# A hybrid LRU/GLA layer on one core: the kernel's scheduler takes a longer figure for split-precision matmuls

## The chip, the cores and the metric

One core of a Trainium2 chip runs the whole program in one launch. The metric is the device time in microseconds; the median of three runs is given. The engines are TensorE (PE in the profile, its weight loads PEld), VectorE (DVE), ScalarE (ACT), GpSimd (POOL) and SyncE (SP), which issues most DMAs.

## The reference, cut to what matters

One layer is applied to two token groups (128 prompt tokens and 512 latent tokens, 640 in all, width 1024), with shared weights:

```python
h = rmsnorm(x, ng[0]) * (1.0 + sc1) + sh1          # sc, sh, g: from silu(c) @ w_mod
z = h @ w_in                                        # 1024 x 7200
zx, zg, q, k, v, g, lr, ga, gb = split(z)
xc = conv4(zx); hf, hb = rg_lru_scan(xc) in both directions   # block-diagonal gates, sigmoid, exp, sqrt, scan
y_a = ((hf + hb) * gelu(zg)) @ lru_up
o = gla_chunked(q, k, v, decay from lr) in both directions, 4 heads
y_b = (rmsnorm(o) * silu(g)) @ gla_up
m = (sigmoid(ga) * y_a + sigmoid(gb) * y_b) @ w_out
x = x + g1 * rmsnorm(m, ng[1])
h = rmsnorm(x, ng[2]) * (1.0 + sc2) + sh2
x = x + g2 * rmsnorm(square(relu(h @ mlp_w1)) @ mlp_w2, ng[3])
```

Besides the tokens, the final LRU and GLA states of the prompt are returned. Everything is float32.

## The kernel before

All large matrix products are done in split precision: a float32 operand is cast to the type fp32r (its high half: `whi`, `HH`, `ah`) by ScalarE, VectorE subtracts that from the original (its low half: `wlo`, `HL`, `al`), and three matmuls on fp32r operands (high x high, high x low, low x high) are summed in PSUM. The 640 tokens are the columns of most matmuls, as two halves of 320; the v projection has 256 columns, the output projection and the second MLP product 512. Weights come as 1 MB loads into two `raw` tiles and are split into four `whi`/`wlo` buffers.

The program is first recorded and only then issued. The function `tile_hybrid_layer` calls engine operations through `Port` objects; each call becomes an `Op` in the `Recorder`. The recorded order is a list of units, one for each weight piece: first the startup (modulation, norms, transposes), then the input projection with its zx, q, k, v, g, zg pieces, the gates and up-projections, the output projection (`out_pass`), and the MLP (`w1_units`, `w2_units`). Between the units' halves the planner `slot` puts stages of side chains: `lru_chain` (operand split `xs`, gate matmuls into `aux` PSUM tiles, sigmoid reads `r`, exchange by DMA, tanh, exp, sqrt, scans), `gla_chain` (heads, in nine stages), the modulation chains, and the splits of the results. `dense` and `aux` are two PSUM pools of two tiles each: unit results and side-chain results. The planner's budgets are constants (`us=0.01 * (c1 - c0)`, `FILL`) and don't use the lengths that this change touches.

Then `Recorder.order` (L222) makes the order in which every engine gets its instructions. It is a list scheduler: it simulates the five engines in time, with a length for each instruction from `Recorder.cost` (L133), a lag between engines, tile buffers that come free, table switches of ScalarE (`SWITCH_US`, 1.28 us) and a slower TensorE where it has been idle. At each step the engine that can start first takes, of its instructions that are ready, the one of lowest rank (its place in the recorded order; weight splits get a lead of `SPLIT_AHEAD` places; ScalarE prefers instructions that need no table switch). `issue` (L331) then issues all instructions in the order of these simulated times, and on the chip each engine runs its queue in that order, waiting for semaphores where its data isn't there yet. All instructions are recorded as being of line L340, so the profile is read by tile names.

Of the kernel before, what the change touches and what calls it, by code (L numbers as in the profile page):

```python
# [56 lines left out]
def _dims(ap):  # L57
    n = 1
    for _, k in ap.ap[1:]:
        n *= k  # L60
    return n
# [48 lines left out]
class Recorder:  # L110
# [21 lines left out]
    @staticmethod  # L132
    def cost(eng, name, args, kw, out):  # L133
        n = _dims(out)
        if eng == "PE":
            if name == "transpose":
                return max(0.05, n * 2 / 2400)
            if args[1].dtype == F32R:
                return max(n / 2400 + 0.0025, 0.106)
            if out.ap[0][1] <= 32 and n >= 128:  # L140
                return n / 2400 + 0.0025
            return max(0.213, n * 4 / 2400)
        aps = [a for a in list(args[1:]) + list(kw.values()) if hasattr(a, "ap")]
        scalars = sum(_dims(a) == 1 for a in aps) if n > 1 else 0
        sbuf = all(a.space == bass.MemoryType.SB for a in aps)
        if eng == "ACT":
            if name == "dma_start":
                return 0.1
            return (0.093 if sbuf else 0.051) + n / 1200 + 0.094 * scalars
        if eng == "DVE":  # L150
            if name == "reciprocal":
                return 6.25e-3 * n
            fast = name in ("tensor_copy", "tensor_scalar", "memset") and sbuf and out.space == bass.MemoryType.SB
            return 0.068 + n / (1920 if fast else 960) + 0.061 * scalars
        if eng == "POOL":
            if name == "dma_start":
                return 1.0
            if name in ("memset", "affine_select"):
                return 0.03 + n * 0.0009
            if name == "tensor_copy":  # L160
                return 0.1 + n * 0.0034
            return 0.1 + n * (0.008 if name == "tensor_scalar" and n < 64 else 0.0022) + (0.35 if kw.get("op") == OP.pow else 0.06)
        return 0.63 if kw["in_"].space == bass.MemoryType.SB else 0.5
# [1517 lines left out]
```

## Time and profile before

| | us |
|---|---|
| median of 3 runs | 1164.29 (1162.61 to 1165.95) |
| the profiled execution: its time | 1160.65 |
| the profiled execution: its span, first to last instruction | 1158.9 |
| TensorE busy in the span | 1131.3 |
| VectorE, ScalarE, GpSimd busy | 755.6, 557.8, 80.1 |

The span is shorter than the execution's own time by 1.75 us, which lies around the first and last instruction. A matmul's shown length is longer than the distance to the next one, because matmuls overlap; the distance is read from a run of many. "Idle before" is the time in which an engine had nothing running, and behind the arrow stands what ended it.

### The profile page before, as it was taken

To read this page: it belongs to the slowest core of one execution; us is meant where nothing else is said; L and a number is where in the kernel's file an instruction comes from. 1 tells how busy PE (TensorE), PEld (TensorE's weight loads), DVE (VectorE), ACT (ScalarE), POOL (GpSimd) and SP (SyncE) were. 2 spreads that over 40 slices of the span, in tenths; PEclk is the share of its full clock that TensorE was granted. 3 is DMA by queue.
4 is the path that set the end of the run, shared out by engine and by line. 5 is a ranking of instruction groups with operands and counts; after the bars stand their busy time and mean duration, and the time that the engine had idled before them with its cause. 6 is when DMAs were issued, how large, how long until landed. Compare 5 with 4: busy or idle time off the path is not lost.

```text
span 1158.9 us, 17719 instructions
## 1 busy us (share of the span) xinstructions
PE 1131.3 (98%) x7188; PEld 1064.3 (92%) x7188; DVE 755.6 (65%) x1147; ACT 557.8 (48%) x882; POOL 80.1 (7%) x152
## 2 busy tenths in 40 slices
PE   6999999999999999999999999999999999999996
PEld 5899899999999999999999879999999989999995
DVE  4687885966557557549968389885444555555546
ACT  6387989994657668213432388422222222222222
POOL 3135112000000000000000021000000000000001
PEclk9999999999999999999999999999999999999999
DMA  9835445332121312245535356532222222222202
GB/s 296 253 78 142 132 110 132 93 104 77 52 92 40 102 60 83 64 158 207 191 128 182 112 179 199 192 118 74 73 73 74 73 73 73 78 81 86 85 1 90
DMA packets 101009, 130.63 MB, mean 113 GB/s; under 512 B 7790, under 2 KB 77632, under 8 KB 100928
## 3 DMA queue, kind: packets, MB, share of 16 engines
q1 hardware_dynamic: 98880, 127.61, 35.6%
q0 software_dynamic: 2048, 1.90, 0.7%
q8 instruction: 56, 0.92, 0.3%
q14 instruction: 25, 0.20, 0.1%
HBM read 117.94 MB, written 3.68 MB: 105 GB/s over the span
## 4 chain that ended last, share of the span: by engine, by line
PE 78%; DVE 8%; ACT 5%; DMA 5%; issue 2%; POOL 1%; SPq 0%; DVEq 0%; POOLq 0%; ACTq 0%
PE dense L340 62%; PE aux L340 16%; DVE i L340 2%; DVE th L340 2%; DMA i<-r 1%; DVE wlo L340 1%; DMA modw<-in_w_mod_dram 1%; ACT L340 1%; ACT r L340 1%; ACT th L340 1%; DMA raw<-in_w_in_dram 1%; DMA w2raw<-in_gla_w_dram 1%; DMA r<-r 1%; ACT whi L340 1%; ACT L339 0%
## 5 line engine op out<-in xcount | busy, mean ns | idle before, releaser
L340 ACT CAST whi<-raw 128x1024 fp32r<-128x1024 f32 (+1 forms) x159 | 164.5, 1038 | 394.2 <-PE dense L340 363.6
L340 DVE TENSOR_TENSOR wlo<-raw,whi 128x1024 fp32r<-128x1024 f32 x154 | 188.1, 1223 | 173.5 <-ACT whi L340 173.1
L340 PE MATMUL dense<-HH,whi 128*128 128x320 f32 x768 | 178.1, 312 | 0.2 <-ACT vc L340 0.2
L340 PE MATMUL dense<-HL,whi 128*128 128x320 f32 x768 | 176.1, 310 | 0.0
L340 PE MATMUL dense<-HH,wlo 128*128 128x320 f32 x752 | 172.4, 309 | 0.0
L340 PEld LDWEIGHTS dense<-HH,whi 128*128 128x128 f32 x768 | 128.4, 188 | 2.1 <-issue 0.8
L340 PEld LDWEIGHTS dense<-HL,whi 128*128 128x128 f32 x768 | 128.9, 188 | 0.0
L340 PEld LDWEIGHTS dense<-HH,wlo 128*128 128x128 f32 x752 | 125.9, 188 | 0.0
L340 PE MATMUL dense<-H2H,whi 128*128 128x320 f32 (+2 forms) x496 | 116.8, 309 | 0.0
L340 PE MATMUL dense<-H2H,wlo 128*128 128x320 f32 (+2 forms) x496 | 116.4, 308 | 0.0
L340 PE MATMUL dense<-H2L,whi 128*128 128x320 f32 (+2 forms) x496 | 116.4, 308 | 0.0
L340 PEld LDWEIGHTS dense<-H2H,whi 128*128 128x128 f32 x496 | 84.5, 188 | 1.3
L340 PEld LDWEIGHTS dense<-H2L,whi 128*128 128x128 f32 x496 | 84.0, 188 | 0.0
L340 PEld LDWEIGHTS dense<-H2H,wlo 128*128 128x128 f32 x496 | 84.0, 188 | 0.0
L340 DVE SCALAR_TENSOR_TENSOR mac<-mw,cst,mac 128x512 f32<-128x512 f32 x112 | 77.9, 747 | 2.9 <-DMA mw<-in_w_mod_dram 2.7
L340 PE MATMUL dense<-wlo,ah 128*128 128x512 f32 (+1 forms) x192 | 75.3, 392 | 0.0
L340 PE MATMUL dense<-whi,ah 128*128 128x512 f32 (+1 forms) x192 | 75.3, 392 | 0.0
L340 PE MATMUL dense<-whi,al 128*128 128x512 f32 (+1 forms) x192 | 75.3, 392 | 0.0
L340 PE MATMUL aux<-wlo,ah 128*128 128x512 f32 (+1 forms) x132 | 51.7, 392 | 0.0
L340 PE MATMUL aux<-whi,ah 128*128 128x512 f32 (+1 forms) x132 | 51.7, 391 | 0.0
L340 PE MATMUL aux<-whi,al 128*128 128x512 f32 (+1 forms) x132 | 51.6, 391 | 0.0
L340 PE MATMUL dense<-whi,HH 128*128 128x256 f32 x160 | 45.0, 281 | 0.0
(311 smaller groups left out, 2172.6 us busy)
## 6 DMA issues: line engine op xcount, KB each, us to landing
raw<-in_mlp_w_dram SPq DMA_DIRECT2D x34, 1024.0 KB, 5.7
raw<-in_w_in_dram SPq DMA_DIRECT2D x24, 1024.0 KB, 5.5
mw<-in_w_mod_dram SPq DMA_DIRECT2D x64, 256.0 KB, 5.6
modw<-in_w_mod_dram SPq DMA_DIRECT2D x32, 256.0 KB, 6.1
raw<-in_w_out_dram SPq DMA_DIRECT2D x8, 1024.0 KB, 4.9
i<-r SPq DMA_DIRECT2D x32, 160.0 KB, 2.6
raw<-in_w_in_dram SPq DMA_DIRECT2D x8, 512.0 KB, 4.0
raw<-in_lru_up_dram SPq DMA_DIRECT2D x4, 1024.0 KB, 5.1
```

Source lines behind the costliest of these rows:

```text
L340: getattr(eng[o.eng], o.name)(*o.args, **o.kw)
```

## The change

`Recorder.cost` returns the planned length in microseconds of one instruction; `n` is the number of columns. For a matmul on fp32r operands it returns another figure:

```diff
             if name == "transpose":
                 return max(0.05, n * 2 / 2400)
             if args[1].dtype == F32R:
-                return max(n / 2400 + 0.0025, 0.106)
+                return max(n / 2200, 0.106)
             if out.ap[0][1] <= 32 and n >= 128:
                 return n / 2400 + 0.0025
             return max(0.213, n * 4 / 2400)
```

Nothing else differs: the same operations are recorded, in the same recorded order, on the same engines and tiles. What can differ is the order in which `order` lets each engine run them, the DMA issues of SyncE and GpSimd among them.

## Rows read from the trace of the kernel before

**Rows 1.** The page's first part: busy time, share of the span, instructions.
```profile
PE 1131.3 (98%) x7188; PEld 1064.3 (92%) x7188; DVE 755.6 (65%) x1147; ACT 557.8 (48%) x882; POOL 80.1 (7%) x152
```
**Rows 2.** Busy time by stretches: PE, PEld, DVE, ACT, POOL, clock, DMA.
```profile
0.00:50.00 50.00, 38.99 (x311) 31.62 (x312) 28.14 (x81) 25.28 (x62) 11.21 (x40) 0.90 0.94 291
...
100.00:265.00 165.00, 160.19 (x1148) 158.41 (x1146) 126.53 (x181) 149.64 (x182) 18.69 (x32) 1.00 0.41 112
265.00:675.00 410.00, 408.91 (x2759) 398.64 (x2758) 268.24 (x405) 198.02 (x359) 11.28 (x9) 1.00 0.35 113
675.00:700.00 25.00, 23.24 (x115) 18.66 (x114) 22.36 (x41) 21.01 (x40) 5.79 (x5) 1.00 0.51 152
700.00:1150.00 450.00, 449.98 (x2521) 407.00 (x2519) 267.71 (x374) 130.16 (x187) 4.90 (x7) 1.00 0.28 89
1150.00:1158.90 8.90, 0.00 (x0) 0.00 (x0) 3.59 (x8) 1.00 (x4) 1.44 (x2) 0.71 0.39 118
```
**Rows 3.** TensorE's waits, whole run: total us, times, longest.
```profile
PE aux L340 <- ACT r L340: 2.9, 3, 1.7
...
PE aux L340 <- DVE xs L340: 1.7, 1, 1.7
...
PE dense L340 <- DVE wlo L340: 0.8, 1, 0.8
PE aux L340 <- DVE nst L340: 0.7, 1, 0.7
PE aux L340 <- DVE nrm L340: 0.6, 1, 0.6
...
PE aux L340 <- DVE ab L340: 0.4, 1, 0.4
PE aux L340 <- ACT nrm L340: 0.4, 1, 0.4
```
**Rows 4.** Chain pieces (320, then 512 columns); then TensorE's groups, 100 to 265 us.
```profile
473.31 63.46 PE dense L340 x432
...
642.75 2.80 PE aux L340 x12
...
L340 PE MATMUL dense<-HL,whi 128*128 128x320 f32 x246 | 56.2, 309 | 0.0
...
L340 PE MATMUL dense<-whi,HH 128*128 128x256 f32 x110 | 30.7, 279 | 0.0
L340 PE MATMUL dense<-wlo,HH 128*128 128x256 f32 x109 | 30.4, 279 | 0.0
...
L340 PE MATMUL aux<-xs,bh 128*128 128x320 f32 x48 | 11.6, 323 | 4.6 <-ACT r L340 2.9 <-DVE xs L340 1.7
```
**Rows 5.** ScalarE's groups from 100 to 265 us: busy us, mean ns, idle.
```profile
L340 ACT ACT_TABLE_LOAD x22 | 28.2, 1283 | 0.4
L340 ACT CAST whi<-raw 128x1024 fp32r<-128x1024 f32 x20 | 20.9, 1048 | 3.5 <-PE dense L340 2.7 <-DMA raw<-in_w_in_dram 0.8
L340 ACT ACTIVATE r<-aux,C 128x640 f32<-128x640 f32 x24 | 18.2, 791 | 0.4 <-PE aux L340 0.3
L339 ACT ACT_TABLE_LOAD x12 | 15.4, 1283 | 0.2
```
**Rows 6.** VectorE's groups from 100 to 265 us.
```profile
L340 DVE TENSOR_TENSOR wlo<-raw,whi 128x1024 fp32r<-128x1024 f32 x20 | 24.4, 1220 | 12.3 <-ACT whi L340 12.3
L340 DVE TENSOR_TENSOR_SCAN i<-r,C,th 128x512 f32<-128x512 f32 x16 | 20.3, 1269 | 0.0
```
**Rows 7.** The chain of waits by line: 100 to 265 us, then 265 to 460.
```profile
by line: DVE i L340 16.7%; DVE th L340 11.4%; issue 9.5%; PE dense L340 8.2%; DMA i<-r 8.0%; ACT L340 6.2%; ACT r L340 5.6%; DVE wlo L340 4.9%; ACT th L340 4.8%; DMA r<-r 4.5%; ACT whi L340 2.3%; DVE xs L340 2.0%; DVE ab L340 1.7%; ACT L339
...
by line: PE dense L340 66.2%; PE aux L340 25.1%; ACT ab L340 1.8%; issue 1.4%; DVE wlo L340 1.2%; DVE ab L340 1.1%; DVE la L340 0.8%; ACT L339 0.7%; DVE zg L340 0.6%; DVE i L340 0.6%; DVE ep L340 0.4%; DVE ex L340 0.2%; DVE bm L340 0.1%; DV
```
**Rows 8.** ScalarE's waits from 100 to 265 us.
```profile
ACT whi L340 <- PE dense L340: 2.7, 5, 0.8
ACT zg L340 <- PE dense L340: 2.6, 1, 2.6
```

## The prediction

> **What bounds the kernel now.** I read the page's first part, then the table by stretches, then TensorE's waits, then what is behind them. The first part says that TensorE is busy 98% of the span [rows 1]; VectorE and ScalarE are far below. So the time is the length of TensorE's work and its idle time, and an order of work can only touch the second. The stretches say where it is [rows 2]: 50.00 - 38.99 = 11.0 us in the first 50 us, 165.00 - 160.19 = 4.8 us from 100 to 265 us, 1.1 us from 265 to 675, 1.8 us from 675 to 700, nothing (0.02 us) from 700 to 1150, and the 8.9 us tail after the last matmul.
>
> The stretch from 100 to 265 us is the one to look at. It holds the LRU chains: ScalarE is busy 149.64 of 165 us there, 91% [rows 2]. TensorE's waits in it are four: three times on ScalarE's reads of the gates' PSUM tiles (r), 2.9 us in all, and once on VectorE's operand split (xs), 1.7 us [rows 3]. The chain of waits through this stretch is VectorE, ScalarE and DMA; dense matmuls are 8.2% of it [rows 7]. From 265 to 460 us, where the GLA chains run, it is the reverse: dense and aux matmuls are 66.2% and 25.1% [rows 7], and the only TensorE waits are two short ones (nst 0.7 us, ab 0.4 us) [rows 3]. From 675 to 700 us, between the output projection and the MLP, TensorE waits for the normalised tiles (nrm) and once for a low half of a weight (wlo) [rows 3].
>
> **The change part by part.** No instruction is added or removed. A matmul on split-precision operands of 320 columns was planned at 320/2400 + 0.0025 = 0.1358 us and is now planned at 320/2200 = 0.1455 us; of 256 columns 0.1092 and 0.1164; of 512 columns 0.2158 and 0.2327. Of 128 columns it stays at the floor of 0.106. The trace's lengths: 63.46 us for 432 matmuls of 320 columns is 146.9 ns each, 2.80 us for 12 of 512 columns is 233 ns [rows 4]. So the new figures are right to 1%, and the old ones were 7 to 8% short.
>
> The Trainium skill speaks against this: "TensorE: Matmul & The Clock Gate", section on the back-to-back issue gap, gives N/2.4 + 2.5 ns for a warm array, which is the old formula to the digit. By it the LRU stretch's matmuls would be 147 us long, TensorE's idle time there would be 18 us and not 4.8, the helpers alone would set the pace, and the whole 10.25 us worked out below would be lost (1175). The trace does not agree: 146.9 ns, and 160.19 us of work.
>
> What the plan does with the number: it walks all engines in simulated time, and each engine takes the first instruction in program order that is ready at that moment. An aux matmul whose operands or PSUM tile are not ready is passed by dense matmuls. With matmuls planned longer, fewer dense ones fit while a helper works, so aux matmuls move forward in TensorE's queue, which on the chip is then followed as it stands. Whether that is good hangs on how true the helpers' planned lengths are, and the trace shows that they are short too. ScalarE: a weight cast is planned at 0.093 + 1024/1200 = 0.946 us and takes 1.048; a gate sigmoid is planned at 0.051 + 640/1200 + 0.094 = 0.678 and takes 0.791; table loads are planned right (1.28) [rows 5]. VectorE: the low half of a weight is planned at 0.068 + 1024/960 = 1.135 and takes 1.220; a scan of 512 is planned at 0.662 and takes 1.269 [rows 6]. So before, everything was planned about 8 to 15% short, TensorE like the rest; the relative error on ScalarE was small. With 34 loads of 1.283 us right and the other 106 us some 13% short (between the cast's 11% and the sigmoid's 17%), ScalarE's 149.6 us were planned as 137.4, 9% short, against 160.19 / 147.2 = 9% for TensorE. Afterwards TensorE is planned right, and the helpers alone are planned short. The plan then expects them earlier, measured in matmuls, than they come.
>
> Term 1, the LRU stretch. It has 1148 matmuls, all split-precision [rows 2]: 110 + 109 + 109 = 328 of 256 columns (two groups of 109, one shown) and 820 of 320 columns [rows 4]. Old plan 820 x 0.1358 + 328 x 0.1092 = 147.2 us, new plan 820 x 0.1455 + 328 x 0.1164 = 157.4 us: 10.25 us more by the unrounded formulas. If the helpers set every position of an aux matmul, they come due 10.25 us of matmuls earlier by the end of the stretch, and TensorE idles 10.25 us more: the upper bound. If they come in program order, ready in time, nothing moves: 0. The 48 gate matmuls of one kind make 24 PSUM tiles [rows 4], and TensorE waited at 4 of them [rows 3]; 4/24 of 10.25 is 1.7 us, and 92% (the chain without dense matmuls [rows 7]) is 9.4 us. I take 3 us, nearer to the first, because at 20 of 24 tiles TensorE found its data ready; some of these have less slack than the shift and will join the four. Queued behind a waiting aux matmul are all dense matmuls, and with them the evacuations and weight casts, so the loss is not made up later: behind 700 us TensorE has no idle time to give back.
>
> Term 2, 675 to 700 us. 115 matmuls [rows 2], 16.9 ns more for one of 512 columns: 1.9 us at most. Two groups of transposes (nrm) waited, 0.6 and 0.4 us [rows 3]; I take half of that, 0.5 us. Term 3, the GLA stretch: helpers hold 100 - 66.2 - 25.1 = 8.7% of the chain, 17 us of 195; 6.6% of that is 1.1 us at most, and I take 0.2.
>
> Costed at nothing: the start, where TensorE works on float32 transposes and modulation sums and on the DMAs behind them, whose planned lengths stay, with the first split-precision matmuls put between (I allow 1 us either way); the MLP, where TensorE never waits and VectorE is busy 268 of 450 us [rows 2], so a split that comes a few us later is still in time; without that cover each late low half would cost about the 0.8 us of the one wait seen [rows 3]. The tail hangs on the last units alone.
>
> Sum: 3.0 + 0.5 + 0.2 = +3.7 us on the profiled execution's 1160.65, 1164.35; the median of the runs shown is 3.64 us above that execution, so 1168.0 in its terms.
>
> **The rivals.** (a) Nothing that can be measured. The order shifts, but slack takes it up: 20 of 24 gate tiles were not waited for, and the chain is TensorE itself outside the LRU stretch. Terms of 0 to 1.5 us: about 1165. Against it: a list order is never moved by exactly nothing, and ScalarE at 91% has little slack. That the order comes out the same on every engine, so that the change does nothing, belongs here too; since every matmul's planned end moves, I hold it for unlikely.
>
> (b) Faster. ScalarE's queue is in order too: in the LRU stretch it stood idle 2.7 us before weight casts and 2.6 us before a zg copy, waiting for dense matmuls that the old plan thought done [rows 8]. With true matmul lengths these go later in ScalarE's queue, and gate reads that stood behind them go earlier. If ScalarE gets those 5.3 us back and the LRU chains end that much sooner, TensorE's 4.8 us of waits there go, and perhaps 1 us at 675: 1164.3 - 5.8, about 1158.5. It decides where the gate reads come more than 1 us earlier, since the mean wait is 4.6/4. Against it: VectorE's scans, planned at half their length, are just as late as before, and one of the four waits is VectorE's.
>
> (c) Slower by more: table switching. 34 table loads take 43.6 us of the stretch [rows 5]. A plan that thinks ScalarE less loaded finds fewer instructions waiting at once and switches more often. Five loads more are 6.4 us on an engine with 15 us to spare. With term 1 that gives 1171 to 1175. It is the upper half of the slower case.
>
> **How the numbers follow.** About 0.3%, 3.5 us, is what a measurement of this kernel can tell from no change. Slower by more, by terms 1 to 3 with or without (c): 0.45, and the likeliest time is 1168. Within it, (a): 0.35. Faster, (b): 0.20. My terms' upper bounds, 10.25 + 1.9 + 1.1 = 13.3 us, give 1177.6; all waits behind 50 us gone, 4.8 + 1.1 + 1.8 = 7.7 us, gives 1156.6. The range of 1158 to 1175 leaves out the outer edges of both. The slower case by itself is 1167 to 1176.
>
> **What would show it.** TensorE's busy time should stay at 1131 us and its matmul count at 7188. Right would be: idle time from 100 to 265 us of 7 to 9 us where it was 4.8, behind gate matmuls that wait for r or xs, and the last LRU step (nst) with fewer dense matmuls ahead of it. The stretch from 700 to 1150 us should be unchanged. Wrong would be fewer than 4.8 us there with ScalarE's waits for dense matmuls gone (b), the same waits at other places (a), or new waits in the MLP for wlo, which I count at nothing. A count of table loads far from 53 would speak for or against (c).

## The result and the profile after

The median went from 1163.51 us (1162.61 to 1165.95, 4 runs, one more than in the table above) to 1184.72 us (1182.5 to 1185.5, 4 runs): a ratio of 1.0176, with a 95% interval of 1.0154 to 1.0197. The change is slower, by 21 us. The forecast was slower by 3.7 us and the range ended at 1175, so the sign came out and the size did not. The profiled execution took 1184.93 us with a span of 1183.2, that is 24.3 us more than the span of before.

The page's first part of the changed kernel, to be held against [rows 1], and its line of ScalarE's table loads at one of the two places that issue them:

```profile
PE 1137.8 (96%) x7188; PEld 1067.9 (90%) x7188; DVE 755.7 (64%) x1147; ACT 569.5 (48%) x891; POOL 80.7 (7%) x152
...
L340 ACT ACT_TABLE_LOAD x43 | 55.2, 1283 | 1.5 <-PEq L1668 0.8
```

TensorE ran the same 7188 matmuls and was busy 6.5 us longer; the other 17.8 us are idle time. ScalarE has 9 instructions more (891 against 882). These are table loads: the page shows 43 here where that of before has 34, and 19 at the other place (L339) in both. VectorE and GpSimd did the same work.

The stretches of the changed kernel, cut so that they hold about the work of [rows 2] (the columns are the same):

```profile
0.00:50.00 50.00, 37.35 (x302) 30.03 (x303) 27.62 (x80) 25.43 (x62) 10.20 (x38) 0.90 0.94 282
50.00:100.00 50.00, 48.65 (x329) 47.74 (x328) 33.09 (x55) 32.58 (x51) 30.53 (x61) 1.00 0.38 101
100.00:284.00 184.00, 165.91 (x1145) 163.01 (x1143) 135.43 (x191) 162.03 (x195) 18.62 (x32) 0.97 0.41 110
284.00:696.00 412.00, 409.59 (x2772) 399.52 (x2773) 263.90 (x399) 194.90 (x353) 8.90 (x7) 1.00 0.35 112
696.00:722.00 26.00, 24.19 (x117) 19.15 (x116) 23.83 (x43) 20.85 (x41) 6.57 (x6) 1.00 0.47 138
722.00:1173.00 451.00, 450.79 (x2521) 407.36 (x2520) 267.50 (x375) 132.48 (x188) 4.66 (x7) 1.00 0.28 90
1173.00:1183.20 10.20, 1.35 (x12) 1.15 (x10) 4.33 (x11) 1.29 (x6) 1.22 (x2) 0.69 0.34 103
```

Some 1145 matmuls of the LRU stretch now take 184 us, where 1148 took 165. TensorE's idle time by stretch, against [rows 2]: 12.7 us at the start (11.0), 1.4 from 50 to 100 us (the stretch that [rows 2] leave out had none), 18.1 in the LRU stretch (4.8), 2.4 in the GLA stretch (1.1), 1.8 in the transition (1.8), 0.2 in the MLP (0.02), and a tail of the same length. So 13.3 of the 17.8 us lie in the LRU stretch. The granted clock has fallen to a mean of 0.97 there; it was 1.00.

TensorE's waits over the whole run of the changed kernel, against [rows 3]:

```profile
PE aux L340 <- ACT r L340: 10.1, 6, 3.2
PE dense L340 <- ACT zp L340: 5.1, 3, 2.9
...
PE aux L340 <- DVE nst L340: 1.8, 1, 1.8
PE aux L340 <- DVE ab L340: 1.7, 2, 1.0
PE dense L340 <- ACT vc L340: 1.4, 1, 1.4
PE aux L340 <- DVE nrm L340: 1.4, 1, 1.4
```

Gate matmuls wait for ScalarE's reads (r) 10.1 us in place of 2.9. New is that dense matmuls wait 5.1 us for ScalarE's evacuation of a dense tile (zp), which [rows 3] don't have at all. Both point at ScalarE, so its waits come next. From 75 us to the last LRU step (nst, at 284 us) they are in the changed kernel:

```profile
ACT th L340 <- POOL p4sp L340: 6.4, 1, 6.4
ACT th L340 <- DMA r<-r: 5.6, 1, 5.6
ACT va L340 <- PE dense L340: 4.2, 1, 4.2
ACT whi L340 <- PE dense L340: 3.5, 5, 0.8
```

and in the kernel before, over the same work (75 to 266 us, which begins 25 us ahead of [rows 8]):

```profile
ACT whi L340 <- PE dense L340: 7.3, 7, 4.4
ACT zg L340 <- PE dense L340: 2.6, 1, 2.6
...
ACT th L340 <- DMA r<-r: 0.9, 2, 0.4
```

Waits for dense matmuls are not what grew: they are 7.7 us in all, and were 10.3 (with 0.4 for va). What is new stands elsewhere. Twice a tanh (th) stands at the head of ScalarE's queue before its data is there, once for a constant that GpSimd makes (p4sp) and once for the exchange by DMA (r). These two are 12.0 us, where the kernel before has 0.9. The timeline of ScalarE in the changed kernel shows the first of them, and what follows (start, us, engine, line, operation, and in brackets the idle time ahead of it):

```profile
86.38 0.73 ACT L340 CAST xs<-xc 64x640 fp32r<-64x640 f32 x1
93.48 1.55 ACT L340 ACTIVATE th<-r,p4sp 128x640 f32<-128x640 f32 x2 [6.38 <-POOL p4sp L340]
95.05 1.28 ACT L339 ACT_TABLE_LOAD   x1
96.34 1.55 ACT L340 ACTIVATE r<-r,n8sp 128x640 f32<-128x640 f32 x2
97.79 0.63 ACT L340 COPY zp<-dense 128x192 f32<-128x192 f32 x2
...
100.22 1.28 ACT L340 ACT_TABLE_LOAD   x1
101.51 0.83 ACT L340 ACTIVATE th<-r,p4sp 128x640 f32<-128x640 f32 x1
102.36 1.28 ACT L340 ACT_TABLE_LOAD   x1
```

In the kernel before the four tanhs stand together, later in the queue and with no wait ahead of them:

```profile
101.38 2.99 ACT L340 ACTIVATE th<-r,p4sp 128x640 f32<-128x640 f32 x4
```

Two tanhs were placed earlier, and a third alone behind them. ScalarE stands still for 6.4 us, then switches tables for one or two instructions at a time, and the copies and casts behind them are late.

### The profile page after: what moved, and what is told of

Read it like the earlier page. It is cut to its first block, busy times and chain, and to the rows that moved or that the text cites. A ratio compares the mean times of both kernels' runs of the same rounds, so it can differ in the third digit from the quotient of the medians.

```text
span 1183.2 us, 17745 instructions
## 1 busy us (share of the span) xinstructions
PE 1137.8 (96%) x7188; PEld 1067.9 (90%) x7188; DVE 755.7 (64%) x1147; ACT 569.5 (48%) x891; POOL 80.7 (7%) x152
## 4 chain that ended last, share of the span: by engine, by line
PE 72%; ACT 12%; DVE 5%; DMA 4%; issue 4%; POOL 2%; SPq 0%; ACTq 0%; DVEq 0%; POOLq 0%
PE dense L340 58%; PE aux L340 14%; ACT L340 3%; DMA modw<-in_w_mod_dram 2%; ACT r L340 2%; ACT th L340 1%; ACT whi L340 1%; ACT L339 1%; POOL spp L340 1%; DMA i<-r 1%; ACT ab L340 1%; DVE i L340 1%; DMA raw<-in_w_in_dram 1%; DVE wlo L340 1%; ACT zg L340 1%
## 5 line engine op out<-in xcount | busy, mean ns | idle before, releaser
L340 PEld LDWEIGHTS dense<-HH,whi 128*128 128x128 f32 x768 | 129.5, 190 | 10.1 <-ACT zp L340 5.9
```

What stands on the lines that cost most here:

```text
L340: getattr(eng[o.eng], o.name)(*o.args, **o.kw)
```

## Did the gate matmuls move in TensorE's queue?

The prediction said that aux matmuls come forward past dense ones. Whether they did can be read from counts: the matmuls that were run from the start to a given gate tile. In the kernel before, gate tiles begin at 204.41, 225.74 and 232.28 us; up to just before these:

```profile
0.00:204.40 204.40, 190.50 (x1387) 182.25 (x1388) 143.84 (x247) 154.47 (x231) 56.66 (x130) 0.97 0.57 162
0.00:225.73 225.73, 211.60 (x1527) 202.80 (x1528) 165.07 (x278) 173.94 (x255) 56.66 (x130) 0.98 0.55 153
0.00:232.27 232.27, 216.46 (x1559) 207.40 (x1559) 171.61 (x291) 180.43 (x263) 56.66 (x130) 0.98 0.55 155
```

In the changed kernel gate tiles begin at 221.04, 243.05 and 251.12 us:

```profile
0.00:221.03 221.03, 194.94 (x1387) 184.63 (x1388) 148.56 (x254) 166.06 (x241) 59.35 (x130) 0.96 0.53 150
0.00:243.04 243.04, 215.72 (x1527) 205.16 (x1528) 167.29 (x285) 186.68 (x267) 59.35 (x130) 0.96 0.51 144
0.00:251.11 251.11, 220.58 (x1559) 209.75 (x1559) 175.11 (x295) 194.65 (x276) 59.35 (x130) 0.97 0.52 146
```

1387, 1527 and 1559 matmuls stand ahead in both kernels. These three gate tiles didn't move in TensorE's queue; they are reached 16.6, 17.3 and 18.8 us later. Of the 18.8, 14.7 are idle time (30.53 - 15.81) and 4.1 longer busy time for the same 1559 matmuls. On ScalarE 276 instructions were run by then and not 263, in 14.2 us more of busy time.

Not all gate tiles stayed. There are 32 of them, of four matmuls each; counted in the same way and taken in order, 20 have as many matmuls ahead as before, 11 have fewer (by 2 to 120) and one has more (by 12). The furthest move is that of two tiles side by side, of which the first began at 160.41 us and begins at 153.40 now; the last LRU step (nst) moved too. Up to just before the tile and before nst, in the kernel before:

```profile
0.00:160.40 160.40, 146.71 (x1067) 138.91 (x1068) 113.51 (x208) 116.54 (x186) 47.34 (x114) 0.97 0.58 166
0.00:265.84 265.84, 249.38 (x1799) 240.03 (x1799) 194.55 (x324) 207.66 (x296) 56.66 (x130) 0.98 0.53 148
```

and in the changed one:

```profile
0.00:153.39 153.39, 131.94 (x947) 122.48 (x948) 100.27 (x189) 104.50 (x171) 47.35 (x110) 0.96 0.59 168
0.00:284.21 284.21, 251.91 (x1772) 240.78 (x1772) 196.35 (x325) 220.04 (x307) 59.35 (x130) 0.96 0.49 138
```

So aux matmuls did come forward, as the prediction said: 120 matmuls for these two tiles, 27 for nst. But most of the wait isn't there. TensorE's timeline has the gate tiles' waits for r, in the last brackets; three of the six are:

```profile
129.65 0.56 PE L340 MATMUL aux<-xs,bh 128*128 128x320 f32 x2 [1.31 <-ACT r L340]
...
193.21 0.56 PE L340 MATMUL aux<-xs,bh 128*128 128x320 f32 x2 [2.71 <-ACT r L340]
...
251.12 0.56 PE L340 MATMUL aux<-xs,bh 128*128 128x320 f32 x2 [3.21 <-ACT r L340]
```

The first is a tile that came forward (by 10 matmuls), the other two stayed. Of the 10.1 us, 3.7 are at three tiles that came forward (1.3 at 129.65, 1.8 at 142.90 and 0.5 at 144.30 us), where the kernel before waited 2.7 us (1.0 for r, 1.7 for xs); 6.4 are at three that stayed (2.7, 0.5 and 3.2). The two tiles that moved by 120 aren't waited for at all. The rest of the 18.1 us in the LRU stretch is 6.4 us before dense matmuls and 1.6 before nst.

## The experiments

Four theories were set against each other. **R** (proportion): what counts is whether the planned lengths of the engines stand in proportion; a true matmul among helpers that are planned short puts the in-order queues out of step with one another. **Q** (ScalarE's queue): the loss is in that queue alone, in its waits at the head and its table loads. **D** (the prediction): positions of aux matmuls in TensorE's queue. **L** (luck): any other order of instructions would have cost as much, the one of before was a lucky one. Ratios are against the kernel before, run on the same chip.

**One engine's queue kept.** Two plans are made; one engine's order is taken from the first and forced on the second:

```diff
+        kept = {e: [o.idx for o in self.plan(first, {}) if o.eng == e] for e in ('ACT',)}
+        return self.plan(second, kept)
```

Run 1 has ScalarE's order as before and plans the rest with the new figure:

> New matmul figure, but ScalarE's queue is kept in the order that the old plan gave it (53 table loads); all other queues are planned around it with the new figure. Theory Q (the loss sits in ScalarE's queue: nine more table loads, 9 x 1.283 = 11.5 us, and two waits at the head of its queue, 6.4 and 5.6 us): within 5 us of the kernel before, 1160 to 1168. Theory D (my prediction's term 1: TensorE's own queue has aux matmuls too early, because the helpers alone are planned short): TensorE's queue is still of the new figure, so 1178 to 1186 stays.

Run 2 has the old figure, and ScalarE's order as in the changed kernel:

> Old matmul figure, but ScalarE's queue is kept in the order that the new plan gave it (62 table loads); all other queues are planned around it with the old figure. Theory Q: the loss comes without the change, 1178 to 1188. Theory D: TensorE's queue is planned with the old figure, so 1163 to 1168.

Run 3 has TensorE's order as before, and the rest with the new figure:

> New matmul figure, but TensorE's queue is kept in the order that the old plan gave it; the others are planned around it with the new figure, which gives ScalarE 57 table loads. Theory D: the loss goes, 1162 to 1167. Theory Q: ScalarE's order is still a new one, four table loads more than before (5.1 us) and whatever head waits it has, so 1169 to 1183.

| run | median us | ratio, interval | table loads |
|---|---|---|---|
| 1 ScalarE as before | 1172.21 | 1.0075 (1.0053 to 1.0096) | 53 |
| 2 ScalarE as after | 1179.57 | 1.0136 (1.0119 to 1.0152) | 62 |
| 3 TensorE as before | 1176.99 | 1.0114 (1.0095 to 1.0134) | 57 |

ScalarE's order carries most of the loss and not all: with the order of before 43% of the loss is left (0.75 of 1.76), and the order of after brings 77% of it to queues that are otherwise planned with the old figure. (The other queues are planned anew around the one that is kept, so neither run has them as they were.) What is left in run 1 is seen at the gate matmuls, which wait 6.7 us for r though ScalarE's order is the old one:

```profile
PE aux L364 <- ACT r L364: 6.7, 4, 3.3
```

ScalarE itself waits 19.6 us for dense matmuls there, from 75 to 285 us:

```profile
ACT va L364 <- PE dense L364: 10.0, 2, 8.4
ACT whi L364 <- PE dense L364: 9.6, 9, 3.9
```

That is more than in the kernel before (10.3), but run 9 below has nearly as much of it, 17.8 us, and no loss, so it doesn't explain what is left:

```profile
ACT whi L344 <- PE dense L344: 12.5, 10, 3.1
ACT va L344 <- PE dense L344: 5.3, 3, 4.3
```

TensorE's order of before leaves 65% of the loss. In run 3 its gate matmuls wait as they do in the changed kernel, 9.4 us:

```profile
PE aux L364 <- ACT r L364: 9.4, 5, 3.9
```

So theory D doesn't hold for most of it: with its own old order TensorE waits all the same, because what it waits for is late. And Q alone doesn't hold either: the order of before, beside a plan with the new figure, still loses 0.75%. Run 1 lies between the ranges that were set for Q and D; runs 2 and 3 lie in Q's.

**Other lengths brought to the true ones too.** Run 4 keeps the new matmul figure and gives GpSimd's smallest operations, with which it makes the constant p4sp, 0.5 us; run 5 makes all the helpers 7% longer, in step with the matmul:

```diff
             # run 4, GpSimd
+            if n <= 16:
+                return 0.5
...
         # run 5, behind o.us = self.cost(...)
+        if eng in ("ACT", "DVE", "POOL") and name != "dma_start":
+            o.us *= 1.07
```

> New matmul figure, and GpSimd's instructions on 16 columns and fewer (the softplus chain behind the tanh's scale p4sp) planned at 0.5 us, about what the trace shows, where they were planned at 0.2 to 0.3. Nothing else. Theory Q, with its start at the tanh that ScalarE's queue has too early: the plan then puts the tanhs later, the 6.4 us wait goes, ScalarE has 54 table loads and not 62, and the time is 1162 to 1170. Theory D: GpSimd's lengths have no part in it, 1180 to 1186.

> New matmul figure, and ScalarE's, VectorE's and GpSimd's planned lengths times 1.07, so that they stand to TensorE's as in the kernel before. Theory R (what counts is that all engines are planned equally short; the matmul alone made true sets the in-order queues against each other): most of the loss goes, 1160 to 1168, with 48 table loads. Theory L (the old plan's order was a lucky one among many; any other order costs 5 to 20 us): 1170 to 1182.

Run 4: 1175.96 us, ratio 1.0106 (1.0088 to 1.0124). The wait for p4sp is gone and 54 table loads are left of 62, yet 60% of the loss stays: less than D's range has and more than Q's. Run 5: 1165.48 us, 1.0021 (1.0007 to 1.0035), 48 loads: 88% of the loss is taken back, with the new matmul figure in place. This lies in R's range.

**Size of the step, and luck.** Run 6 takes `n / 2300`, halfway in the divisor: a matmul of 320 columns is planned 3.3 ns longer than before, where the change adds 9.6. Run 7 takes `n / 2050`, which adds 20.3 ns. Run 8 keeps the old figure and gives each helper instruction a fixed pseudo-random error of up to 3% either way:

```diff
+        o.us *= 1 + 0.03 * (((o.idx * 2654435761 + 1 * 40503) >> 7) % 1024 / 511.5 - 1)
```

> The matmul planned at n / 2300, about half of the change's step (0.139 us for 320 columns, between 0.136 and 0.1455); 53 table loads in the plan. Theory R: about half of the loss, 1170 to 1176. Theory L: no relation to the step's size, anywhere from 1163 to 1185.

> The matmul planned at n / 2050, longer than it is (0.156 us for 320 columns), twice the change's step; 59 table loads in the plan. Theory R: the helpers stand still shorter against TensorE, more is lost than by the change, 1186 to 1200. Theory L: no relation, 1165 to 1185.

> Old matmul figure; each length of ScalarE, VectorE and GpSimd is off by a fixed pseudo-random share between -3% and +3%, with no bias. 58 table loads in the plan, 5 more than before. Theory R: no bias, so little is lost beyond the table loads, 1162 to 1170. Theory L: another order, another 5 to 20 us, 1169 to 1184.

| run | median us | ratio, interval | table loads |
|---|---|---|---|
| 6 3.3 ns added | 1164.71 | 1.0016 (1.0003 to 1.0028) | 53 |
| 7 20.3 ns added | 1199.9 | 1.0315 (1.0293 to 1.0338) | 59 |
| 8 random errors, old figure | 1163.14 | 1.0004 (0.9994 to 1.0014) | 58 |

For 3.3, 9.6 and 20.3 ns the loss is about 2, 21 and 37 us: it grows with the step, and the first third of the step costs less than its share (7 us). Run 6 is a miss for R, which was set to lose 1170 to 1176 there. The order of run 8 is another one, like those of runs 5 and 6, and it costs nothing that can be measured, so theory L falls. It doesn't show by itself that the direction counts: its errors are at most 3% where the change is 7%, and run 6, one-sided by 2.4% for 320 columns, costs hardly more. Run 8 also speaks against Q: it has 58 loads, and the same tanh at the head of ScalarE's queue, at no cost that can be measured. From its ScalarE waits, 75 to 285 us:

```profile
ACT th L342 <- POOL p4sp L342: 5.3, 1, 5.3
```

Here such a wait and five more loads are taken up by the slack. That in the changed kernel it is the sum of many small delays that isn't would fit, and isn't shown.

**All lengths true, and one engine at a time.** Run 9 has the new matmul figure and helpers' lengths read from the trace:

```diff
-            return (0.093 if sbuf else 0.051) + n / 1200 + 0.094 * scalars
+            return (0.195 if sbuf else 0.160) + n / 1200 + 0.094 * scalars
...
-            return 0.068 + n / (1920 if fast else 960) + 0.061 * scalars
+            if name == "tensor_tensor_scan":
+                return 0.13 + n / 460
+            return 0.155 + n / (1920 if fast else 960) + 0.061 * scalars
```

and GpSimd as in run 4. Runs 10 and 11 are run 5 with the factor for ScalarE alone and for VectorE alone. Run 12 leaves the matmul at the old figure and divides the helpers' lengths by 1.07: the same proportion as in the changed kernel, without its edit. Run 13 has the helpers of run 9 beside the old matmul figure, the opposite error.

> New matmul figure, and the helpers' lengths set to about what the trace shows: ScalarE 0.195 or 0.160 + n/1200 us where it was 0.093 or 0.051 + n/1200, VectorE 0.155 + n/960 where it was 0.068 + n/960, scans 0.13 + n/460, GpSimd 0.5 us up to 16 columns. 53 table loads in the plan. Theory R: with every length true the loss of the change is gone, and, since the helpers are now a little longer against TensorE than in the kernel before, 1156 to 1166. The rest of theory Q (ScalarE's queue order, whatever the lengths): 1164 at best. A theory by which a longer matmul figure costs by itself: 1180.

> New matmul figure, and ScalarE's planned lengths alone times 1.07. 60 table loads in the plan, 7 more than before. If the loss comes from ScalarE planned too fast against TensorE: 1164 to 1171, in spite of the table loads. If it comes from VectorE planned too fast: 1178 to 1186. If from both: between, 1171 to 1178.

> New matmul figure, and VectorE's planned lengths alone times 1.07. 54 table loads in the plan. If the loss comes from VectorE: 1164 to 1171. If from ScalarE: 1178 to 1186. If from both: 1171 to 1178.

> Old matmul figure, and ScalarE's, VectorE's and GpSimd's planned lengths divided by 1.07: the matmul isn't touched, but the helpers stand to it as after the change. 65 table loads in the plan. Theory R: the loss comes without the change, 1178 to 1192. A theory by which it is the matmul's figure itself: 1162 to 1168.

> Old matmul figure with the helpers' lengths set to what the trace shows: the helpers are now planned long against TensorE, the error of the change turned round. 48 table loads in the plan. If only helpers planned too short cost (data that the queues expect too early): no loss, 1157 to 1165, and perhaps a gain of a few us on the kernel before. If any error in the relative lengths costs: 1170 to 1180.

| run | median us | ratio, interval | table loads |
|---|---|---|---|
| 9 all true | 1161.87 | 0.9991 (0.9976 to 1.0006) | 53 |
| 10 ScalarE in step | 1179.38 | 1.0137 (1.0113 to 1.0161) | 60 |
| 11 VectorE in step | 1174.14 | 1.0093 (1.007 to 1.0115) | 54 |
| 12 old matmul, helpers shorter | 1180.11 | 1.0145 (1.0125 to 1.0165) | 65 |
| 13 old matmul, helpers true | 1168.29 | 1.0049 (1.0034 to 1.0063) | 48 |

Run 12 makes 82% of the loss without the edit, with the same picture in TensorE's waits:

```profile
PE aux L342 <- ACT r L342: 10.7, 4, 4.4
```

Run 9 has the edit and no loss. TensorE is idle 0.8 us in the LRU stretch, less than the 4.8 of [rows 2]:

```profile
100.00:265.00 165.00, 164.23 (x1189) 163.51 (x1187) 128.81 (x181) 147.69 (x182) 20.58 (x36) 1.00 0.42 114
```

This doesn't show in the total: its interval holds 1, so no version here is shown to be faster than the kernel before. Bringing ScalarE alone into step gives back 22% of the loss and VectorE alone 47%; both with GpSimd 88% (run 5). Run 10 lies in the range that was set for VectorE as the only cause, run 11 in that for both; since neither factor alone gives back what run 5 does, both have a part. The opposite error (run 13) costs 5 us, between the two ranges that were set for it, and not in this place: its LRU stretch has 160.16 of 165 us busy, as before.

**Where the plan goes wrong.** Run 14 uses the new figure only for matmuls recorded ahead of head 2's v projection, which is recorded about where the LRU chains end; run 15 only from there on:

```diff
         if u.tag == "v2":
+            rec.early, rec.late = False, True
```

> The new figure only for the matmuls recorded before the v projection of head 2 (about the first 240 us, with nearly all of the LRU chains), the old one behind it. 62 table loads in the plan, as after the change. If the loss is made in the LRU stretch: 1180 to 1186. If it is spread over the GLA stretch and the passage to the MLP too: 1172 to 1179.

> The reverse of the run before: the old figure up to the v projection of head 2, the new one behind it, for three quarters of all matmuls. 53 table loads in the plan. If the loss is made in the LRU stretch: 1162 to 1167. If it is spread: 1168 to 1175.

Run 14: 1180.35 us, ratio 1.0141 (1.0119 to 1.0163), 62 loads. Run 15: 1166.29 us, 1.0023 (1.0007 to 1.0039), 53 loads. So 80% of the loss is made by the matmuls up to the LRU chains' end and 13% by all those behind.

**Where the loss is seen in all runs.** One wait goes with it throughout: that of gate matmuls for r. It is 0.5 to 4.8 us in the kernel before and in runs 5, 6, 8, 9, 13 and 15, whose ratios go up to 1.0049, and 6.7 to 11.9 us in the changed kernel and in the other nine, whose ratios begin at 1.0075. The ends of both groups are runs 9 and 15, and run 1 (above) and 7:

```profile
PE aux L344 <- ACT r L344: 0.5, 1, 0.5
...
PE aux L343 <- ACT r L343: 4.8, 3, 3.1
...
PE aux L340 <- ACT r L340: 11.9, 4, 6.3
```

This says where the delays of the helpers reach TensorE, not how they come about.

## Why the prediction was wrong in size

**What held.** Slower; the place (the LRU stretch holds 13.3 of 17.8 us of the new idle time, and run 14 makes 80% of the loss); no change in the MLP (450.79 us busy of 451); the waits at gate matmuls for r; the last LRU step with fewer dense matmuls ahead of it (1772 matmuls in place of 1799); and the starting point, that with this edit the helpers alone are planned short, which runs 5, 9 and 12 show from three sides.

**The step that failed: Term 1.** It took all idle time of the stretch to come from aux matmuls that come forward in TensorE's queue, bounded it by the 10.25 us of planned matmul time that the edit adds there, and took 3 us; what the edit does to the other queues stood in no term. The stretch lost 13.3 us, more than the bound. The mechanism is there in part: 11 of 32 gate tiles came forward. But the waits at those tiles are 3.7 us, 1.0 us more than before, and with TensorE's order of before 65% of the loss is left (run 3). Most of it came about in the other queues, ScalarE's above all (run 2: its order alone brings 77%). That queue was put in order for a time at which GpSimd and the exchange were thought further on: waits of 6.4 and 5.6 us at its head for p4sp and r; ten more table loads by the tile at 251 us (42 against 32: 12.8 us of its 14.2 us of longer busy time; nine more over the whole run); and behind it gate tiles that hadn't moved and wait 6.4 us for r, and dense matmuls that wait 5.1 us for zp. None of these was in the sum.

The prediction's comparison of planned and true lengths also left out GpSimd, and called everything "about 8 to 15% short", though by its own figures a scan is planned at 0.662 us and takes 1.269. Bringing GpSimd's smallest operations alone nearer to their length takes back 40% of the loss (run 4).

**Terms 2 and 3** were of the right kind, Term 3 too small: no change of idle time in the transition (1.8 us both times; 0.5 was forecast), and 1.3 us more in the GLA stretch (0.2 was forecast, and the bound was 1.1). The start and the stretch up to 100 us, costed at nothing with 1 us allowed, lost 1.6 + 1.4 us of idle time.

**TensorE's busy time** was to stay at 1131 us and rose to 1137.8. Part of that is the clock (below), which no term had.

**The rivals.** (c), more table switches, had the right sign and the right engine, with 5 more loads where there were 9; but loads alone are not the cause, since 58 loads cost nothing in run 8 and 54 with 1.0106 in run 4. (b), ScalarE getting its waits for matmuls back, came true in its first half: over the same work they are 7.7 us in place of 10.3, and none is left for zg. But the waits for p4sp and r, 12.0 us in place of 0.9, took more than that. (a), slack that takes it up, is true of the first third of the step (run 6) and not of the whole.

**What stays open.** How the loss is divided between head waits, table loads and engines that wait for each other in turn; a wait at ScalarE's head, more table loads and a wait of dense matmuls for zp (3.6 us) were all seen in run 8 without loss. And why a third of the step costs 2 us and the whole 21: that slack is used up in between would fit, and wasn't shown by itself.

## What to carry to other kernels

In a plan that several in-order queues follow, the proportion between the engines' planned lengths can count more than the truth of any one of them: here a 7% correction of TensorE's figure alone cost 1.8%, and the same correction on the helpers too left 0.2%. Correct such figures together, or not at all, and before forecasting an order, look at every engine's queue, not that of the bounding engine alone: count the instructions ahead of a late one in both kernels, and if the counts agree, what it waits for is late. Count them for all the late ones: here some had moved and some had not. Small random errors in a plan can be harmless (up to 3% in run 8).

## What was not expected of the hardware

Three of TensorE's waits in the changed kernel, of 2.9, 2.7 and 3.2 us, were each followed by a stretch at half clock. The timeline of TensorE shows the first wait, and the stretches show the clock behind it (the column ahead of the last two) beside the stretch that follows:

```profile
114.52 0.56 PE L340 MATMUL dense<-HH,whi 128*128 128x320 f32 x2 [2.89 <-ACT zp L340]
```

```profile
115.30:118.70 3.40, 3.40 (x15) 3.40 (x14) 3.40 (x6) 3.37 (x5) 0.00 (x0) 0.51 0.03 7
119.00:122.40 3.40, 3.40 (x25) 3.40 (x24) 3.34 (x6) 3.38 (x4) 0.00 (x0) 1.00 0.00 0
```

In 3.4 us TensorE, busy all the while, ran 15 matmuls at the granted 0.51 (the level of 1.2 GHz) and 25 at 1.00 (2.4 GHz). Ten matmuls fewer, at some 0.14 us, is 1.4 us for this wait on top of its 2.9. The third (clock 0.52, 14 matmuls in 3.4 us from 252 us) costs about as much, the second (0.60, and partly idle) somewhat less: some 4 us in all, of the 6.5 us by which TensorE was busy longer. The rest of the 6.5 wasn't traced. [rows 3] have no wait of more than 1.7 us in the LRU stretch, and the clock there was 1.00 [rows 2]. So the first of these waits, on the engine that sets the pace, cost half again its length.
